# The products of a sample pair with cached values: one key tile for both samples at a time, instead of four key tiles of one sample and then of the other

## The chip, the cores and the metric

The program runs on one core of one Trainium2 chip. The metric is the device time of that core in microseconds (us). The kernel before took 3969.97 us, the median of three runs (3956.18 to 3974.96).

## What is computed

One layer of a hybrid encoder is computed for two groups that share all weights: a prompt of 2048 rows and eight samples of 16 rows each. Each layer projects its input, runs four mixers, adds the result back and ends with a feed-forward block. Three of the four mixers (B, C and D) are attentions. For the samples each has a cache of keys and values from the past, 1024 rows for B and C, 512 for D. Cut to what matters here, for mixer C:

```python
kc = jnp.concatenate([cache['fox_k'], kc], axis=1)      # 1024 cached rows, 16 new ones
vc = jnp.concatenate([cache['fox_v'], vc], axis=1)
...
p = jax.nn.softmax(jnp.where(mask, s, -jnp.inf), axis=-1)
return jnp.einsum('bhqk,bkhd->bqhd', p, v32)
```

The change is in the last product, weights by values, for the samples alone. All numbers are float32.

## The kernel before

The work falls into a dense stream (projections, then the feed-forward block of four parts of the prompt) and a stream of mixers. Both are written as generators. `weave` (line 144) takes a step of the mixers and then dense steps for as long as the mixer's pace says. The result is handed to a scheduler, which fixes the order of each engine's queue before the program runs. An engine then works its own queue strictly from front to back and waits where an operand is missing. All loads and stores stand in one such queue, that of SyncE (SP). In it, too, stand empty instructions that `Order.note` puts there (line 97): each waits for an earlier dense product, and a later dense product waits for it, so a held SP queue can hold TensorE (PE).

The samples' attention runs in three stages, one for each of B, C and D (`attn_samples`, line 1498, called by `mixers`), beside the delta-rule steps of the prompt and the dense stream. `samples_steps` handles the eight samples in four pairs. For a pair, `weights` makes the attention weights, 128 rows: sample `u` of the pair has rows 64u to 64u+63, four heads of 16 queries. Then `values` (line 1602)

- turns the weights into `swT`, one 128x128 tile for each key tile of 128 keys,
- makes the product with the 16 new rows (tile `sxv`) as one full 128-column product, and
- adds the products with the cached values (tile `cv`) in the same PSUM tile, which has the name `ptr`. Each takes 64 columns of `swT` as stationary operand, so sample 0 works in columns 0 to 63 of the array, sample 1 in columns 64 to 127, and both over all 128 rows; 256 value columns stream through.

With `nk` key tiles (8 for B and C, 4 for D) there are 2 x nk products for a pair: 64 in B, 64 in C, 32 in D. They are made in groups of four key tiles:

```python
for s in range(nk // 4):
    for u in range(2):
        v = load(b + u, cv, s, "cv")
        for j in range(4):
            kt = 4 * s + j
            K.pe.matmul(po[64 * u:64 * u + 64, :256], wT[:, kt, 64 * u:64 * u + 64], v[:, j], start=False, stop=(kt == nk - 1))
        yield
```

`load` (line 1549) fetches four key tiles of one sample, 512 KB, from the cache to the tile `cv`, of which there is one buffer, so each load waits for the last product of the group before. The keys have their own tile `ck`, loaded by the same line 1552. `K.pe.matmul` is line 107 in every profile, and `K.pe.transpose` line 110. In the rows below, `d` is the PSUM tile of dense products, and `wu` and `wd` are the weights of the feed-forward block. A float32 product leaves two records on PE, one for each of two passes. A float32r product leaves one.

Elsewhere in the program, `solve` (lines 1319 and 1359) makes four products for the delta rule whose outputs `pw` take turns between the lower and the upper 64 columns (`<-lA,kbv` in the rows); their moving operand has 128 columns.

Of the kernel before, what the change touches and what calls it, by code (L numbers as in the profile page):

```python
# [5 lines left out]
F32 = mybir.dt.float32  # L6
# [3 lines left out]
AF = mybir.ActivationFunctionType  # L10
ALU = mybir.AluOpType
# [4 lines left out]
P = 128  # L16
# [656 lines left out]
def logf_stage(K, part):  # L673

    nc, tc, I, O = K.nc, K.tc, K.I, K.O
    a, b = 4 * part, 4 * part + 4
    with tc.tile_pool(name="lf", bufs=1, side="right", reuse_waits="tile") as sp:
        bf = sp.tile([P, 4], F32, name="bf")
        nc.sync.dma_start(out=bf, in_=I["fox_b_f"].to_broadcast([P, 4]))
        for c, n in [(slice(a, b), 4)] + ([(slice(NP, NT), 1)] if part == 0 else []):  # L680
            x = sp.tile([P, n, 4], F32, name=f"fx{n}")
            nc.vector.tensor_tensor(x, K.fl[:, c], bf.unsqueeze(1).to_broadcast([P, n, 4]), op=ALU.add)
            yield
            sn = sp.tile([P, n, 4], F32, name=f"fsn{n}")
            nc.vector.tensor_scalar(sn, x, 0.0, None, op0=ALU.min)
            l1 = yield from softplus_tail(K, sp, x, [P, n, 4], f"f{n}")
            nc.vector.tensor_tensor(K.logf[:, c], sn, l1, op=ALU.subtract)
        nc.sync.dma_start(out=O["fox_logf_p"].rearrange("(t p) h -> p t h", p=P)[:, a:b], in_=K.logf[:, a:b, :])
        if part == 0:
            nc.sync.dma_start(out=O["fox_logf_s"], in_=K.logf[:, NP, :])  # L690
        yield
        lf = K.logf[:, 0:b, :].rearrange("p t h -> p (t h)")
        n = 4 * b
        pt = K.mps("z")
        K.pe.matmul(pt[:, :n], K.tri, lf, start=True, stop=True)
        po = K.mps("z")
        K.pe.matmul(po[:, :n], K.ones, lf, start=True, stop=True)
        tot = sp.tile([P, b, 4], F32, name="ftot")
        nc.vector.tensor_copy(tot, po[:, :n].rearrange("p (t h) -> p t h", h=4))
        yield  # L700
        inc = sp.tile([P, b, 4], F32, name="finc")
        for h in range(4):
            nc.vector.tensor_tensor_scan(out=inc[:, :, h], data0=tot[:, :, h], data1=K.zeros[:, :b], initial=0.0, op0=ALU.add, op1=ALU.add)
        yield
        nc.vector.tensor_tensor(inc, tot, inc, op=ALU.subtract)
        nf = sp.tile([P, n], F32, name="nf")
        nc.vector.tensor_tensor(nf, inc.rearrange("p t h -> p (t h)"), pt[:, :n], op=ALU.subtract)
        yield
        pf = K.mps("z")
        K.pe.transpose(pf[:n, :P], nf, K.ident)  # L710
        nft = sp.tile([P, P], F32, name="nft")
        nc.vector.tensor_copy(nft[:n], pf[:n, :P])
        nc.sync.dma_start(out=K.nF[4 * a:n], in_=nft[4 * a:n])


def softplus_tail(K, sp, x, shape, tag):

    nc = K.nc
    u = sp.tile(shape, F32, name=tag + "u")
    nc.scalar.activation(u, x, AF.Abs)  # L720
    nc.scalar.activation(u, u, AF.Exp, scale=-1.0)
    yield
    w = sp.tile(shape, F32, name=tag + "w")
    nc.vector.tensor_scalar(w, u, 1.0, None, op0=ALU.add)
    l = sp.tile(shape, F32, name=tag + "l")
    nc.scalar.activation(l, w, AF.Ln)
    yield
    e = sp.tile(shape, F32, name=tag + "e")
    nc.vector.tensor_scalar(e, w, 1.0, None, op0=ALU.subtract)
    nc.vector.tensor_tensor(e, u, e, op=ALU.subtract)  # L730
    nc.vector.reciprocal(w, w)
    nc.vector.tensor_tensor(e, e, w, op=ALU.mult)
    nc.vector.tensor_tensor(l, l, e, op=ALU.add)
    yield
    return l
# [762 lines left out]
def attn_samples(K, g, beside):  # L1498

    A = Ctx()  # L1500
    A.ev, A.wb, A.pb, A.sb = Eng(K.nc, 0.5), 2, 2, 1
    A.psum = lambda: K.mps("ptr")
    A.w = lambda m: A.sp.tile([P, P], F32, name="wn", bufs=1) if m <= P else A.sp.tile([P, 512], F32, name="w", bufs=A.wb)
    with K.tc.tile_pool(name="s" + g, bufs=1, side="right", reuse_waits="tile") as A.sp:
        yield from merge((lab(K.nc, "s" + g, samples_steps(K, A, g)), 1.0), (beside, 1.0))


def samples_steps(K, A, g):
    nc, I, sp, psum = K.nc, K.I, A.sp, A.psum
    gi = "BCD".index(g)  # L1510
    name = {"B": "sb", "C": "fox", "D": "band"}[g]
    ck, cv = I[f"cache_{name}_k"], I[f"cache_{name}_v"]
    nk = 4 if g == "D" else 8
# [3 lines left out]
        segs = segs[::-1]  # L1517
    x0 = []
    for n, src in (("k", K.qs[g]), ("v", K.ks[g])):
        t = sp.tile([P, 4, 256], F32, name="c" + n, bufs=1)[:, 0]  # L1520
        nc.sync.dma_start(out=t, in_=src)
        x0.append(t)
    qn, kn = x0
# [8 lines left out]
    if g == "D":  # L1532
        bias = sp.tile([P, 640], F32, name="sbias", bufs=1)
        for h in range(8):
            r = slice(h * 16, h * 16 + 16)
# [3 lines left out]
    pt = psum()  # L1539
# [3 lines left out]
    for o in range(2):  # L1543
        r = slice(o * 64, o * 64 + 64)
# [1 line left out]
    nc.scalar.copy(kT0.rearrange("p x n -> p (x n)"), pt[:, 256:512])  # L1546
    yield

    def load(b, src, s, tag):

        t = sp.tile([P, 4, 256], F32, name=tag, bufs=1)
        nc.sync.dma_start(out=t, in_=src[0, b, s * 512:(s + 1) * 512].rearrange("(t p) h d -> p t (h d)", p=P))
        return t

    def keys(L, b, s):

        L.kT[s] = []
        for u in range(2):
            k = load(b + u, ck, s, "ck")
            kT = sp.tile([P, 2, 512], F32, name="ckT", bufs=2)  # L1560
            L.kT[s].append(kT)
            for x in range(2):
                pt = psum()
                for j in range(4):
                    K.pe.transpose(pt[:, j * P:(j + 1) * P], k[:, j, x * P:x * P + P], K.ident)
                A.ev.copy(kT[:, x], pt)
                yield

    def weights(L, b):
# [21 lines left out]
        for n, (c0, c1) in enumerate(segs):  # L1591
            if c0 < past and c0 // 512 not in L.kT:
                yield from keys(L, b, c0 // 512)
            if g == "B":
                L.w.segment(c0, c1)
            else:
                L.w.segment(n)
            yield
# [3 lines left out]
    def values(L, b):  # L1602
        w, rl = L.w, None if g == "B" else L.w.rl
        wT = sp.tile([P, nk + 1, P], F32, name="swT", bufs=1)
        for a in range(0, nk + 1, 4):
            e = min(a + 4, nk + 1)
            pt = psum()
            for kt in range(a, e):
                K.pe.transpose(pt[:, (kt - a) * P:(kt - a + 1) * P], w(kt), K.ident)
            A.ev.copy(wT[:, a:e].rearrange("p t n -> p (t n)"), pt[:, :(e - a) * P])  # L1610
            yield
        po = psum()
        K.pe.matmul(po[:, :256], wT[:, nk], vn, start=True, stop=False)
        for s in range(nk // 4):
            for u in range(2):
                v = load(b + u, cv, s, "cv")
                for j in range(4):
                    kt = 4 * s + j
                    K.pe.matmul(po[64 * u:64 * u + 64, :256], wT[:, kt, 64 * u:64 * u + 64], v[:, j], start=False, stop=(kt == nk - 1))
                yield  # L1620
        o4 = sp.tile([P, 4, 64], F32, name="so4", bufs=1)
        nc.vector.tensor_tensor(o4, po[:, :256].rearrange("p (h d) -> p h d", d=64), K.hmask.unsqueeze(2).to_broadcast([P, 4, 64]), op=ALU.mult)
        o = sp.tile([P, 64], F32, name="so", bufs=2)
        nc.vector.tensor_reduce(o, o4.rearrange("p h d -> p d h"), axis=AX.X, op=ALU.add)
        if rl is not None:
            nc.vector.tensor_scalar(o, o, rl, None, op0=ALU.mult)
        sq = sp.tile([P, 64], F32, name="sosq", bufs=1)
        ss = K.small.tile([P, 1], F32, name="soss")
        nc.scalar.activation(sq, o, AF.Square, accum_out=ss)
        r = rsqrt(K, K.small, ss, 1, 1.0 / 64, EPS, "rs1")  # L1630
        yield
        nc.vector.scalar_tensor_tensor(o, o, r, mgr, op0=ALU.mult, op1=ALU.mult)
        for u in range(2):
            dst = K.mixed[SEQ + (b + u) * 16:SEQ + (b + u) * 16 + 16, (1 + gi) * 256:(2 + gi) * 256]
            nc.sync.dma_start(out=dst.rearrange("s (h d) -> h s d", d=64), in_=o[64 * u:64 * u + 64])

    L = Ctx()
    L.kT = {}
    s0 = nk // 4 - 1 if g == "B" else 0
    yield from keys(L, 0, s0)  # L1640
    for b in range(0, NB, 2):
        yield from weights(L, b)
# [391 lines left out]
def gates(K, p):  # L2034

    if p:
        yield from gate_stage(K, 4 * p, 4 * p + 4)
    yield from logf_stage(K, p)
    if p == 2:
        yield from fox_cum_samples(K)  # L2040
# [128 lines left out]
```

## Time and profile before

| | |
|---|---|
| runs | 3974.96, 3956.18, 3969.97 us; median 3969.97 |
| the profiled execution, own time | 3970.47 us |
| its span | 3968.7 us |
| granted TensorE clock, mean over the span | 0.966 |
| PE busy | 3688.0 us (93%) |
| PE weight loads (beside PE) | 3176.5 us (80%) |
| DVE, ACT, POOL busy | 2428.5, 1535.7, 1425.6 us |
| moved by DMA | 830.43 MB, 209 GB/s on average |
| stage B of the samples | about 1180 to 1460 us |
| stage C | about 2030 to 2290 us |
| stage D | about 2925 to 3110 us |

The profiled execution lies 0.5 us from the median, so its span can stand for the runs. A granted clock of 1.0 is 2.4 GHz and one of 0.5 is 1.2 GHz; 0.966 is a mean of stretches at either. The three stages are 725 us of the span; the rest is prompt work and the feed-forward block.

### The profile page before, as it was taken

Reading aid. Unit: us, or ns where it says so; the run is one execution under the profiler, and the core shown is the slowest. Engines: PE = TensorE matmul, PEld = TensorE weight load, DVE = VectorE, ACT = ScalarE, POOL = GpSimd, SP = SyncE. Lnnn points to the kernel's source line nnn. Section 1 sums busy time; section 2 is a strip of 40 time slices with the busy share of each in tenths; the row PEclk is TensorE's granted clock in tenths of the full one; section 3 lists DMA queues with packets and bytes.
Section 4 is the critical chain, followed back from the end, with each engine's and each line's share of the span. In section 5 each row is a group of like instructions: output and inputs, shape, how many; then the busy total and the mean of one; then the engine's idle time right before and its main releaser. Section 6 shows DMA issues by size and latency. Waiting matters only on the chain.

```text
span 3968.7 us, 67360 instructions
## 1 busy us (share of the span) xinstructions
PE 3688.0 (93%) x22763; PEld 3176.5 (80%) x22763; DVE 2428.5 (61%) x5592; ACT 1535.7 (39%) x3351; POOL 1425.6 (36%) x3487
## 2 busy tenths in 40 slices
PE   6988899999988998989889999899899999999999
PEld 4987889989975666767766687788777787899999
DVE  5668655464568756867756568666576644354444
ACT  3455323353355424645533245454343222132221
POOL 4456244362433445742232257411232331121112
PEclk7999999999999999999999999999999999999999
DMA  6887968777786876667656654454655645534442
GB/s 223 290 269 245 305 202 297 272 256 259 235 263 209 286 238 237 204 204 260 210 170 202 210 185 147 152 173 155 214 174 200 207 163 188 205 135 146 146 145 92
DMA packets 528445, 830.43 MB, mean 209 GB/s; under 512 B 112011, under 2 KB 350619, under 8 KB 527836
## 3 DMA queue, kind: packets, MB, share of 16 engines
q1 hardware_dynamic: 526629, 825.16, 62.3%
q8 instruction: 181, 2.97, 0.3%
q0 software_dynamic: 1472, 0.97, 0.1%
q14 instruction: 163, 1.34, 0.1%
HBM read 611.81 MB, written 224.16 MB: 211 GB/s over the span
## 4 chain that ended last, share of the span: by engine, by line
PE 66%; DMA 10%; DVE 8%; POOL 3%; ACT 3%; issue 2%; SPq 1%; DVEq 0%; POOLq 0%; ACTq 0%
PE d L107 47%; PE z L107 6%; PE oT L107 5%; PE ptr L110 4%; PE ptr L107 3%; DVE pr L760 1%; DMA add<-nF 1%; PE d L110 1%; DMA w<-win 1%; DMA raw<-in_w_down_dram 1%; DVE wl L860 1%; DVE gy L1203 1%; PE z L110 1%; DMA wu<-keptw_up 1%; DVE cv L1927 1%
## 5 line engine op out<-in xcount | busy, mean ns | idle before, releaser
L107 PE MATMUL d<-hh,wu 128*128 128x512 f32 (+1 forms) x3520 | 1035.9, 368 | 28.9 <-SPq L97 16.2
L107 PEld LDWEIGHTS d<-hh,wu 128*128 128x128 f32 x3520 | 638.9, 191 | 121.1 <-SPq L97 21.7
L107 PE MATMUL d<-w,hh 128*128 128x256 f32 (+2 forms) x3536 | 683.8, 289 | 28.8 <-DVE w L478 9.9
L107 PE MATMUL d<-hl,wu 128*128 128x512 f32 (+1 forms) x1760 | 650.2, 369 | 25.1 <-SPq L97 23.3
L107 PEld LDWEIGHTS d<-w,hh 128*128 128x128 f32 x3536 | 561.4, 192 | 46.7 <-DVE w L478 12.6
L107 PE MATMUL d<-gh,wd 128*128 128x512 f32 (+1 forms) x1760 | 535.4, 371 | 19.6 <-SPq L97 17.7
L107 PE MATMUL d<-w,hl 128*128 128x256 f32 (+2 forms) x1768 | 504.7, 287 | 0.2 <-DVE hl L427 0.2
L1927 DVE SCALAR_TENSOR_TENSOR cv<-u,fcw,cv 128x512 f32<-128x512 f32 (+1 forms) x440 | 299.2, 703 | 201.4 <-ACT cv L1925 199.1
L1837 DVE SCALAR_TENSOR_TENSOR acc<-d,mod,acc 128x512 f32<-128x512 f32 (+2 forms) x432 | 281.9, 656 | 220.8 <-PE d L107 219.4
L107 PEld LDWEIGHTS d<-hl,wu 128*128 128x128 f32 x1760 | 336.0, 191 | 76.5 <-SPq L97 29.9
L107 PEld LDWEIGHTS d<-gh,wd 128*128 128x128 f32 x1760 | 321.6, 191 | 68.9 <-issue 13.5
L107 PEld LDWEIGHTS d<-w,hl 128*128 128x128 f32 x1768 | 338.6, 192 | 4.8 <-issue 3.3
L107 PE MATMUL d<-gl,wd 128*128 128x512 f32 (+1 forms) x880 | 322.0, 366 | 2.1 <-SPq L97 2.0
L1914 ACT COPY u<-d 128x512 f32<-128x512 f32 (+1 forms) x220 | 110.2, 501 | 486.7 <-PE d L107 478.9
L107 PE MATMUL z<-kT,qT 128*128 128x512 f32 (+3 forms) x864 | 257.4, 382 | 16.0 <-DVE mx L792 10.9
L859 ACT CAST wh<-ptr 128x512 fp32r<-128x512 f32 (+1 forms) x372 | 200.6, 553 | 182.6 <-PE ptr L110 104.9
L860 DVE TENSOR_TENSOR wl<-ptr,wh 128x512 fp32r<-128x512 f32 (+1 forms) x372 | 233.2, 637 | 54.0 <-ACT wh L859 49.5
L1929 POOL COPY hal<-u 128x2 f32<-128x2 f32 x176 | 45.6, 259 | 555.8 <-ACT u L1914 547.6
L110 PE MATMUL ptr<-ident,w 128*128 128x128 f32 x1448 | 230.6, 278 | 14.1 <-POOL pr L755 4.4
L760 DVE TENSOR_TENSOR_SCAN pr<-sn,pr,zeros 128x512 f32<-128x512 f32 (+3 forms) x172 | 220.4, 1287 | 37.2 <-ACT sn L752 31.1
L762 POOL TENSOR_TENSOR w<-w,pr 128x512 f32<-128x512 f32 (+3 forms) x168 | 195.0, 1164 | 87.3 <-DVE pr L760 45.7
L792 DVE CUSTOM_DVE_ANT_0 w<-z,add 128x512 f32<-128x512 f32 (+3 forms) x272 | 147.3, 555 | 110.3 <-PE z L107 54.5
(610 smaller groups left out, 7212.1 us busy)
## 6 DMA issues: line engine op xcount, KB each, us to landing
wu<-keptw_up SPq DMA_DIRECT2D x264, 512.0 KB
w<-win SPq DMA_DIRECT2D x132, 512.0 KB
wd<-keptw_down SPq DMA_DIRECT2D x132, 512.0 KB
keptw_up<-wu SPq DMA_DIRECT2D x88, 512.0 KB
wu<-keptw_o SPq DMA_DIRECT2D x48, 512.0 KB
win<-w SPq DMA_DIRECT2D x44, 512.0 KB
raw<-in_w_up_dram SPq DMA_DIRECT2D x88, 256.0 KB
keptw_down<-wd SPq DMA_DIRECT2D x44, 512.0 KB
```

What stands on the lines that cost most here:

```text
L107: return self.note(self.nc.tensor.matmul(out, lhsT, rhs, **k), n / 2400 * (4 if rhs.dtype == F32 else 1))
L110: return self.note(self.nc.tensor.transpose(*a, **k), 0.107)
L760: nc.vector.tensor_tensor_scan(out=pr[:, 0:m][:, ::-1], data0=sn[:, :m][:, ::-1], data1=K.zeros[:r, :m], initial=carry, op0=ALU.mult, op1= ...
L762: nc.gpsimd.tensor_tensor(w[:, :m], w[:, :m], pr[:, 1:m + 1], op=ALU.mult)
L792: nc.vector.tensor_tensor_reduce(out=w[:, :m], in0=ps[:, :m], in1=self.addend(c0, c1), op0=ALU.add, op1=ALU.max, scale=1.0, scalar=-3.0e38 ...
L859: nc.scalar.copy(wh[:, c0:c1], pt[:, c0:c1])
L860: nc.vector.tensor_tensor(wl[:, c0:c1], pt[:, c0:c1], f(wh[:, c0:c1]), op=ALU.subtract)
L1203: nc.vector.scalar_tensor_tensor(yc, tap(c, i), self.cw[:, c, i:i + 1], yc, op0=ALU.mult, op1=ALU.add)
L1837: nc.vector.scalar_tensor_tensor(acc[k][:, c0:m], ps[:, :m - c0], gate[:, k, 0:1], acc[k][:, c0:m], op0=ALU.mult, op1=ALU.add)
L1914: nc.scalar.copy(u[:, 2 + c0:2 + m], ps[:, :m - c0])
L1927: nc.vector.scalar_tensor_tensor(o, tap(i), cw[:, i:i + 1], o, op0=ALU.mult, op1=ALU.add)
L1929: nc.gpsimd.tensor_copy(K.hal[:, fi], tail)
```

## The change

In `values` the loop goes over key tiles. For each one, both samples' rows are fetched in one load of 256 KB (`load_v`), and the two products follow each other, each on its half of the columns, with its tile position written out. `cv` has two buffers of half the size, together the same 512 KB. The number of products, what they multiply and the bytes loaded stay as they are; there are 80 loads of `cv` instead of 40. A step of the generator now covers two key tiles of both samples instead of four of one, so the number of steps is the same.

Two small tiles go away as well: the sum in `logf_stage` is made in place, and the squares in `values` are written over the first quarter of `so4`, which has been read by then.

```diff
@@ logf_stage
-        nf = sp.tile([P, n], F32, name="nf")
-        nc.vector.tensor_tensor(nf, inc.rearrange("p t h -> p (t h)"), pt[:, :n], op=ALU.subtract)
+        nf = inc.rearrange("p t h -> p (t h)")
+        nc.vector.tensor_tensor(nf, nf, pt[:, :n], op=ALU.subtract)
@@ samples_steps
     for n, src in (("k", K.qs[g]), ("v", K.ks[g])):
-        t = sp.tile([P, 4, 256], F32, name="c" + n, bufs=1)[:, 0]
+        t = sp.tile([P, 4 if n == "k" else 2, 256], F32, name="c" + n, bufs=1 if n == "k" else 2)[:, 0]
...
-    def load(b, src, s, tag):
-
-        t = sp.tile([P, 4, 256], F32, name=tag, bufs=1)
-        nc.sync.dma_start(out=t, in_=src[0, b, s * 512:(s + 1) * 512].rearrange("(t p) h d -> p t (h d)", p=P))
-        return t
+    def load(b, s):
+
+        t = sp.tile([P, 4, 256], F32, name="ck", bufs=1)
+        nc.sync.dma_start(out=t, in_=ck[0, b, s * 512:(s + 1) * 512].rearrange("(t p) h d -> p t (h d)", p=P))
+        return t
+
+    def load_v(b, kt):
+
+        t = sp.tile([P, 2, 256], F32, name="cv", bufs=2)
+        nc.sync.dma_start(out=t, in_=cv[0, b:b + 2, kt * P:(kt + 1) * P].rearrange("u p h d -> p u (h d)"))
+        return t
...
-        for s in range(nk // 4):
+        for kt in range(nk):
+            v = load_v(b, kt)
             for u in range(2):
-                v = load(b + u, cv, s, "cv")
-                for j in range(4):
-                    kt = 4 * s + j
-                    K.pe.matmul(po[64 * u:64 * u + 64, :256], wT[:, kt, 64 * u:64 * u + 64], v[:, j], start=False, stop=(kt == nk - 1))
+                r = 64 * u
+                K.pe.matmul(po[r:r + 64, :256], wT[:, kt, r:r + 64], v[:, u], start=False, stop=(kt == nk - 1), tile_position=(0, r))
+            if kt % 2:
                 yield
...
-        sq = sp.tile([P, 64], F32, name="sosq", bufs=1)
         ss = K.small.tile([P, 1], F32, name="soss")
-        nc.scalar.activation(sq, o, AF.Square, accum_out=ss)
+        nc.scalar.activation(o4[:, 0], o, AF.Square, accum_out=ss)
```

The scheduler makes a new order from this. PE's queue, the first block of products in stage B (`sxv` is the product with the new rows, `ck` are key tiles being transposed). Before:

```order
L107 MATMUL ptr<-sxv,swT 128x256
L107 MATMUL ptr<-cv,swT 64x256 x4
L110 MATMUL ptr<-ident,ck 128x128 x4
L107 MATMUL d<-hl,wu 128x512
L107 MATMUL d<-hh,wu 128x512 x2
L107 MATMUL d<-hl,wu 128x512
L107 MATMUL d<-hh,wu 128x512 x2
L107 MATMUL d<-hl,wu 128x512
L107 MATMUL d<-hh,wu 128x512
L107 MATMUL ptr<-cv,swT 64x256 x4
L107 MATMUL d<-hh,wu 128x512
```

And of the change, with the buffers' numbers:

```order
L107 MATMUL ptr_16679<-sxv_16090,swT_16558 128x256
L107 MATMUL ptr_16679<-cv_16681,swT_16558 64x256 x2
L107 MATMUL ptr_16679<-cv_16685,swT_16558 64x256 x2
L107 MATMUL d_17806<-hh_17733,wu_17794 128x512
L107 MATMUL d_17988<-hh_17733,wu_17976 128x512
L107 MATMUL ptr_16679<-cv_16719,swT_16558 64x256 x2
L110 MATMUL ptr_16700<-ident_123,ck_16697 128x128 x4
L107 MATMUL ptr_16679<-cv_16723,swT_16558 64x256 x2
L107 MATMUL d_17806<-hl_17734,wu_17794 128x512
L107 MATMUL d_17806<-hh_17733,wu_17794 128x512 x2
```

Four products of one sample became two products, one of either sample, from one buffer of `cv`. In all 80 cases the two stand next to each other. There are 66 runs of such products in the new order, 52 of one key tile and 14 of two, with other work of PE between them, where before there were 44 runs.

SP's queue at the same place. Before (`keptw_up` is a store, `raw` a load of the dense stream):

```order
L1552 DMA cv<-in_cache_sb_v_dram 128x4x256
L1813 DMA keptw_up<-wu 128x1024
L1552 DMA cv<-in_cache_sb_v_dram 128x4x256
L1810 DMA raw<-in_w_up_dram 128x4x128
L1552 DMA ck<-in_cache_sb_k_dram 128x4x256
L1237 DMA gK<-kbv 128x768
L1248 DMA gQ<-gqet 128x256
L1552 DMA cv<-in_cache_sb_v_dram 128x4x256
```

And of the change:

```order
L1552 DMA ck<-in_cache_sb_k_dram 128x4x256
L1558 DMA cv<-in_cache_sb_v_dram 128x2x256 x6
L1237 DMA gK<-kbv 128x768
L1552 DMA ck<-in_cache_sb_k_dram 128x4x256
L1558 DMA cv<-in_cache_sb_v_dram 128x2x256
L1248 DMA gQ<-gqet 128x256
L1558 DMA cv<-in_cache_sb_v_dram 128x2x256
```

Six loads of `cv`, each of which waits for an earlier pair of products, now stand in a row, and the store and the load that stood between two of them come after.

## Rows read from the trace of the kernel before

**Rows 1.** The page: the span, busy time by engine, the chain that ended last.
```profile
span 3968.7 us, 67360 instructions
PE 3688.0 (93%) x22763; PEld 3176.5 (80%) x22763; DVE 2428.5 (61%) x5592; ACT 1535.7 (39%) x3351; POOL 1425.6 (36%) x3487
PE 66%; DMA 10%; DVE 8%; POOL 3%; ACT 3%; issue 2%; SPq 1%; DVEq 0%; POOLq 0%; ACTq 0%
```
**Rows 2.** Stretches: us, busy us of each engine (instructions), clock, DMA share, GB/s.
```profile
1180.00:1460.00 280.00, 250.75 (x1239) 177.73 (x1238) 199.88 (x418) 122.77 (x233) 114.30 (x204) 0.95 0.77 253
2030.00:2290.00 260.00, 231.89 (x1211) 165.50 (x1210) 156.82 (x409) 82.49 (x176) 71.63 (x194) 0.95 0.64 202
2925.00:3110.00 185.00, 182.59 (x889) 133.58 (x888) 114.01 (x275) 61.71 (x131) 56.20 (x159) 1.00 0.61 204
3110.00:3968.00 858.00, 837.36 (x5106) 770.15 (x5104) 397.89 (x877) 205.60 (x450) 180.20 (x439) 0.98 0.46 158
```
**Rows 3.** Groups of instructions: busy us, mean ns | idle us before, releaser.
```profile
L107 PE MATMUL ptr<-cv,swT 128*64 128x256 f32 x320 | 79.8, 391 | 6.9 <-DMA cv<-in_cache_fox_v_dram 4.1 <-DMA cv<-in_cache_sb_v_dram 2.8
```
**Rows 4.** PE in order of time, stage B: start, us, tiles, records [idle before].
```profile
1245.29 3.29 PE L107 MATMUL ptr<-cv,swT 128*64 128x256 f32 x8
...
1252.58 1.94 PE L107 MATMUL ptr<-cv,swT 128*64 128x256 f32 x8 [1.58 <-DMA cv<-in_cache_sb_v_dram]
1254.45 0.50 PE L107 MATMUL d<-hh,wu 128*128 128x512 f32 x1
...
1266.40 0.63 PE L107 MATMUL d<-hh,wu 128*128 128x512 f32 x2
1266.87 0.39 PE L107 MATMUL d<-hl,wu 128*128 128x512 f32 x1
1267.19 1.94 PE L107 MATMUL ptr<-cv,swT 128*64 128x256 f32 x8
1269.06 0.66 PE L110 MATMUL ptr<-ident,ck 128*128 128x128 f32 x4
1269.47 0.70 PE L107 MATMUL d<-hh,wu 128*128 128x512 f32 x2
```
**Rows 5.** PE in order of time: 64-column products on alternating halves, and alone.
```profile
493.90 0.43 PE L107 MATMUL ptr<-lA,kbv 128*64 128x128 f32 x2
494.27 0.43 PE L107 MATMUL oT<-kbv,lA 128*128 128x64 f32 x2
...
2259.70 0.66 PE L107 MATMUL oT<-lA,kbv 128*64 128x128 f32 x8
2260.29 0.88 PE L107 MATMUL z<-kbv,lA 128*128 128x64 f32 x6
```
**Rows 6.** The chain of waits: start, us, what; loads of 512 KB to `cv`.
```profile
1248.61 3.93 DMA cv<-in_cache_sb_v_dram
2096.77 3.97 DMA cv<-in_cache_fox_v_dram
2220.13 4.67 DMA cv<-in_cache_fox_v_dram
```
**Rows 7.** The chain of waits: weight loads of 256 KB.
```profile
1177.69 3.49 DMA raw<-in_w_o_dram
1304.06 5.41 DMA raw<-in_w_down_dram
1794.67 6.71 DMA raw<-in_w_down_dram
```
**Rows 8.** Waits in stage B: who waited for what, us in total, times, longest.
```profile
PE d L107 <- SPq L97: 11.5, 4, 7.1
...
SPq L97 <- PE d L107: 71.5, 90, 5.9
SPq L1552 <- PE ptr L107: 19.4, 9, 6.6
```
**Rows 9.** The same in stage C.
```profile
PE d L107 <- SPq L97: 7.7, 4, 4.2
...
SPq L97 <- PE d L107: 92.3, 79, 5.0
```
**Rows 10.** The loads of line 1552: duration on SP in ns, least, median, most.
```profile
L1552 SPq DMA_DIRECT2D cv<-in_cache_sb_v_dram x16: 368/384/1042, 1195.7 to 1450.5; - x16
```

More of the change, by code (lines that the diff above doesn't have):

```diff
@@ L1558, in keys @@
         for u in range(2):
-            k = load(b + u, ck, s, "ck")
+            k = load(b + u, s)
             kT = sp.tile([P, 2, 512], F32, name="ckT", bufs=2)
```

## The prediction

> **What bounds the kernel now.** I read the page first. PE is busy for 3688.0 of 3968.7 us, and the chain that ended last runs through PE for 66% [rows 1]. No other engine passes 61%. The changed products lie in the three stages of the samples' attention, so I read those next, by stretch [rows 2]. PE is busy for 250.75 of 280 us in stage B, 231.89 of 260 in C and 182.59 of 185 in D. After D there are 858 us in which PE works for 837.36, on dense work that stands in its queue. So PE time saved in the stages brings that work forward and is kept to the end, unless something else holds PE in the same stage. D leaves almost no room for that. In B and C PE is idle for a tenth of the time, and there the question is what holds it.
>
> Then the products themselves [rows 3]: 320 records, two for each of 160 products, 79.8 us busy, and 6.9 us of idle time in front of them that a load of `cv` ended. How they follow each other is seen in order of time [rows 4]. A group of four products is eight records; it begins at 1252.58 and the next instruction at 1254.45, so a group holds PE for 1.87 us. All eight records are of one sample and use the same half of the columns, and they stand one behind the other: two products after each other cost twice one.
>
> That two halves need not queue is seen elsewhere in this trace [rows 5]. The delta rule's products have 64 columns over all 128 rows, like ours, stream 128 columns instead of 256, and take turns between the halves. Four of them (eight records) hold PE from 2259.70 to 2260.29, 0.59 us. One alone (two records) holds it from 493.90 to 494.27, 0.37 us. Let a product take p to stream and a run e for changing over. One alone is p + e = 0.37. If the four run two by two, 2p + e = 0.59, so p = 0.22 and e = 0.15; if all four queue, 4p + e = 0.59, so p = 0.07 and e = 0.30. Our own groups, whose products do queue, decide: with twice the columns they should take 4 x 2 x 0.22 + 0.15 = 1.91 us by the first and 4 x 2 x 0.07 + 0.30 = 0.86 by the second, and they take 1.87. So products that take turns between the halves run in twos, and ours stream for (1.87 - 0.15) / 4 = 0.43 us each.
>
> **The products.** Before: 160 x 0.43 + 44 runs x 0.15 = 68.8 + 6.6 = 75.4 us. After: 80 pairs x 0.43 + 66 runs x 0.15 = 34.4 + 9.9 = 44.3 us; the runs are counted in the new order of PE, which keeps every pair together. That is **31.1 us less PE time**, 12.4 each in B and C and 6.2 in D. The first group of stage B takes 3.29 us where others take 1.94 [rows 4], at the lower of the two clocks; with fewer products in it, up to 1.4 us more may go. I leave that to the lower end.
>
> **The waits for `cv`.** Before, the one buffer makes each load wait for the last group. Where it gates PE, 512 KB take 3.9 to 4.7 us [rows 6]; PE's idle time from that is 6.9 us in all [rows 3]. After, the load for key tile k+2 starts when pair k is done, so two loads of 256 KB are under way at a time. I went down the new order's twelve blocks (four in each stage). A pair starts when PE reaches it, or when T + 0.1 us have passed since the pair before the last ended, whichever is later; T is the time from issue to landing. The work between is summed with durations of rows: 0.23 for a dense product, 0.41 for four transposes, from 1269.06 to 1269.47 [rows 4]. The tightest block is the first in B: ahead of its third pair PE has only two dense products, ahead of the fourth four transposes, ahead of the fifth five dense products. Summed over the blocks the waits are 1.7 us at T = 2.0, 10.1 at 3.5, 39 at 5.4 and 68 at 6.7. As a test, the same rule with one buffer and T = 4.0 gives 9.3 us for the kernel before, where the trace has 6.9, so it errs on the high side. T has no row here. The lowest I allow is 2.0, half of what 512 KB take. The highest is a weight load of 256 KB that ran late in stage B, 5.41 us [rows 7]. I take **3.5**, from the 256 KB load at 1177.69 that took 3.49, the nearest in size, time and place. That makes 10.1 - 6.9 = **+3.2 us**, with ends at -5.2 and +32.
>
> The Trainium skill, DMA: Bandwidth & Descriptors, section "Anatomy of one DMA", speaks against halving a load: it gives some 2.0 us for each DMA whatever its size, plus bytes / 436e3 us, a fit for another path of issue. By that formula 512 KB would take 3.2 us, where this trace has 3.9 to 4.7, and 256 KB 2.6; the waits would then be an estimated 3.5 us, and the sum 6.6 us lower than mine. I go by the trace.
>
> **SP.** There are 40 more loads to issue at 0.38 us each [rows 10], 15.4 us in 725 us of stages. SP waits for PE in its empty instructions for 71.5 us in B and 92.3 in C [rows 8, 9], and this covers them. Queued behind a waiting load are other loads, stores and those empty instructions; dense products wait for the latter, now 11.5 us in B and 7.7 in C [rows 8, 9]. SP also waits 19.4 us in B for the one buffer of `cv` or `ck` [rows 8]. With two buffers of `cv` a load comes up earlier, but six now stand in a row in the first block, ahead of a store and a weight load. I take 0; if the cover fails the cost is the 15.4 us of issue, and if half of those 19.2 us of PE's waits go, the gain is some 10 us.
>
> **The rest.** The scheduler also moves other instructions in and between the stages, by places and not in number. I cost this at nothing, and keep for it the same ends as for SP. The sum in place and the squares in `so4` keep their engines and sizes: nothing, since the tiles are free by then.
>
> **The sum.** 3970.0 - 31.1 + 3.2 = 3942.1; I say **3942 us**. The profiled execution's own 3970.5 would give 3942.6.
>
> **The rivals.**
>
> *The loads come late* (0.16). Loads of 256 KB in stage B are seen at 5.41 us [rows 7], and DMA is busy 0.77 there [rows 2]. At T = 5.4 the waits are 39 us, 32 more than now, and the time is 3970 - 31.1 + 32 = 3971: no change. Against it: 512 KB of `cv` themselves take 4 us, and half the bytes to the same tile should not take longer.
>
> *The stages keep half* (0.09). In B and C PE waits on other things a tenth of the time; if half of the 24.8 us saved there turns into longer such waits, the time is 3942 + 12.4 = 3954, no change by the bound below. For it: the empty instructions tie PE to SP. Against it: SP's wait in them is for PE, so a faster PE brings SP forward.
>
> *The halves queue* (0.04). The change then does nothing but cut the runs shorter: 160 x 0.43 + 66 x 0.15 = 78.7 us, 3.3 more than before; with the waits, 3970 + 3.3 + 3.2 = 3977. The Trainium skill, TensorE: Matmul & The Clock Gate, section "Part 3: Packing small matmuls — row/col tiling", says that weight loads overlap running products only where the row groups differ, and here both halves use all rows. By that rule the second product would wait for the first. The products at 2259.70 have the same shape over all rows and took 0.59 us where queuing needs 4 x 0.22 + 0.15 = 1.03 [rows 5], so the trace contradicts it for this case.
>
> *Slower: SP's chain of loads becomes the bound* (0.05). Each load of `cv` stands in SP's queue behind a wait for a pair, and weights stand behind it. If loads take 6.71 us, as one weight load did [rows 7], the waits are 68 us, 61 more than before, and the time is 3970 - 31 + 61 = 4000. It decides from T = 6.3 on, where the waits added pass 31 + 20 us. Against it: no load of `cv` gated PE for more than 4.67 us [rows 6].
>
> **How the numbers follow.** The forecast has 0.66. About 0.5%, 20 us, is what a measurement of this kernel can tell from no change: below 3950 is faster, above 3990 slower. The forecast's bulk is faster; its upper edge, with late loads, half-kept stages and queuing halves, is within the bound: faster 0.67, same 0.28, slower 0.05. The range's lower end is 3970.0 - 31.1 - 5.2 - 10 - 1.4 = 3922. Its upper end takes in the late loads, 3971. Left out are queuing halves, slower, and as much again for orders that fall out badly.
>
> **What would show it.** Right: the `cv` products still have 320 records, but the four records of a lone pair hold PE for about 0.58 us, two starting within 10 ns of each other, and their busy time falls by about 30 us. PE's idle time ended by `cv` loads is 2 to 15 us. PE's busy sum falls to about 3657 us and the stretch after stage D keeps its length. Wrong: a pair holds PE for about 1.0 us (halves queue); idle time ended by `cv` of 30 us and more (late loads); PE's waits for the empty instructions of SP grow beyond 19 us in B and C together while the products shrink as said (the stages keep it).

## The result, and the profile after

The changed kernel takes **3935.54 us**, the median of four runs (3932.53 to 3940.53); the kernel before, run beside it, took 3972.47 (3956.18 to 3975.85). The ratio is 0.9925, with a 95% interval of 0.9905 to 0.9945: faster by 0.75%. Forecast were 3942 us and a gain of 28 us; 37 were gained, and the interval of 22 to 38 us holds both. The products did what was forecast, almost to the letter. PE's idle time did not, and the experiments show that it hangs on the scheduler's order more than on anything that the change set out to do.

The page of the changed kernel: span and busy times.

```profile
span 3930.7 us, 67408 instructions
PE 3664.5 (93%) x22763; PEld 3154.7 (80%) x22763; DVE 2431.6 (62%) x5592; ACT 1537.2 (39%) x3352; POOL 1425.6 (36%) x3487
```

Against [rows 1] the span is 38.0 us shorter and PE is busy 23.5 us less, so 14.5 us went from PE's idle time. The groups of instructions of the changed kernel, the row that answers to [rows 3]:

```profile
L107 PE MATMUL ptr<-cv,swT 128*64 128x256 f32 x320 | 52.0, 419 | 7.8 <-DMA cv<-in_cache_sb_v_dram 7.2 <-DMA cv<-in_cache_fox_v_dram 0.3
```

The same 320 records now cover 52.0 us instead of 79.8; one record is no shorter (419 ns against 391). That is overlap. PE in order of time, the first block of stage B and a run of two key tiles later, against [rows 4]:

```profile
1254.23 0.65 PE L107 MATMUL ptr<-cv,swT 128*64 128x256 f32 x4
1254.81 0.50 PE L107 MATMUL d<-hl,wu 128*128 128x512 f32 x1
...
1300.28 1.08 PE L107 MATMUL ptr<-cv,swT 128*64 128x256 f32 x8
1301.29 0.44 PE L110 MATMUL oT<-ident,gqe 128*128 128x128 f32 x2
```

A lone pair holds PE for 0.58 us (1254.23 to 1254.81) and a run of two pairs for 1.01, which are 0.43 + 0.15 and 2 x 0.43 + 0.15, the two prices of the prediction. The two products of the lone pair start 7 ns apart in the trace.

Who waited, in the changed kernel over the whole span: first PE's waits, then SP's.

```profile
PE d L107 <- SPq L97: 49.7, 30, 11.4
...
PE ptr L107 <- DMA cv<-in_cache_sb_v_dram: 7.2, 3, 5.5
```

```profile
SPq L1558 <- PE ptr L107: 39.1, 43, 2.4
```

And in the kernel before, the same lines:

```profile
PE d L107 <- SPq L97: 61.7, 28, 11.2
```

```profile
SPq L1552 <- PE ptr L107: 60.4, 29, 6.6
```

A load of `cv` or `ck` used to hold SP's queue for up to 6.6 us until the single buffer was free; a load of `cv` now holds it for 2.4 at most, and 39.1 us in all. PE's waits for SP's empty instructions fell by 12.0 us. The one is hardly the cause of the other. In stages B and C, where the loads of `cv` stand, those waits were 11.5 and 7.7 us [rows 8, 9] and are now 13.2 and 4.3. The fall lies between stages B and C, where there are no such loads. There, from 1460 to 2030 us before and from 1460 to 2003 after:

```profile
PE d L107 <- SPq L97: 30.7, 18, 10.6
```

```profile
PE d L107 <- SPq L97: 17.8, 13, 10.0
```

A kernel with one buffer and another order ("before, sample 1 first" below) has 17.2 us between these stages as well.

For the comparisons I cut each profile at the issue of stage B's first load of queries, since nothing ahead of it is changed by the work. The stretch from there to the end, before and after (us, PE busy, then the other engines, clock, DMA share, GB/s):

```profile
1185.40:3968.70 2783.30, 2604.93 (x14517) 2166.82 (x14515) 1699.50 (x3750) 1048.99 (x2262) 899.55 (x2005) 0.97 0.56 188
```

```profile
1182.90:3930.70 2747.80, 2576.81 (x14516) 2137.57 (x14514) 1705.82 (x3750) 1050.60 (x2263) 901.82 (x2005) 0.97 0.58 190
```

It is 35.5 us shorter: 28.1 of PE's busy time, and 178.4 - 171.0 = 7.4 of its idle time. The other 2.5 us lie before stage B, which begins anywhere from 1178.7 to 1186.2 us in the kernels that keep SP's empty instructions.

In stage B itself nothing was gained, as far as the number of records tells. From 1180 to 1460 us PE ran 1238 records where it had run 1239 in [rows 2]; it was busy for 7.6 us less, and so idle for 7.6 us more:

```profile
1180.00:1460.00 280.00, 243.13 (x1238) 166.75 (x1237) 199.28 (x418) 124.72 (x235) 115.26 (x214) 0.93 0.76 246
```

### The profile page after: what moved, and what is told of

It is laid out like the page before. It is cut to its first block, busy times and chain, and to the rows that moved or that the text cites. A ratio compares the mean times of both kernels' runs of the same rounds, so it can differ in the third digit from the quotient of the medians.

```text
span 3930.7 us, 67408 instructions
## 1 busy us (share of the span) xinstructions
PE 3664.5 (93%) x22763; PEld 3154.7 (80%) x22763; DVE 2431.6 (62%) x5592; ACT 1537.2 (39%) x3352; POOL 1425.6 (36%) x3487
## 4 chain that ended last, share of the span: by engine, by line
PE 62%; DMA 10%; DVE 10%; POOL 4%; ACT 3%; issue 3%; SPq 1%; DVEq 0%; POOLq 0%; ACTq 0%
PE d L107 45%; PE z L107 5%; PE oT L107 5%; PE ptr L110 4%; PE ptr L107 2%; PE d L110 1%; DVE pr L760 1%; DMA w<-win 1%; DMA add<-nF 1%; DVE acc L1842 1%; DVE gy L1203 1%; DVE wl L860 1%; PE z L110 1%; DMA raw<-in_w_up_dram 1%; DVE cv L1932 1%
## 5 line engine op out<-in xcount | busy, mean ns | idle before, releaser
L107 PE MATMUL d<-w,hh 128*128 128x256 f32 (+2 forms) x3536 | 684.7, 289 | 28.1 <-DVE w L478 9.5
L107 PEld LDWEIGHTS d<-hl,wu 128*128 128x128 f32 x1760 | 334.8, 190 | 66.0 <-SPq L97 17.2
L110 PE MATMUL ptr<-ident,w 128*128 128x128 f32 x1448 | 227.7, 276 | 15.3 <-POOL w L762 3.9
L809 ACT ACTIVATE w<-w,nm 128x512 f32<-128x512 f32 (+3 forms) x284 | 174.1, 616 | 105.6 <-DVE nm L802 82.6
```

The source lines that it names most:

```text
L107: return self.note(self.nc.tensor.matmul(out, lhsT, rhs, **k), n / 2400 * (4 if rhs.dtype == F32 else 1))
L110: return self.note(self.nc.tensor.transpose(*a, **k), 0.107)
L809: self.K.nc.scalar.activation(w, w, AF.Exp, bias=self.nm, accum_out=self.l[:, s:s + 1])
```

## The experiments

Three theories stood at the start. A: the halves run beside each other, and that is the gain. B: the gain lies in the half-sized loads with two buffers. C: the scheduler's new order is lucky. Each profile is split as above; all the numbers stand in one table behind the experiments.

**Both samples on the same half.** The changed kernel, with its loads and buffers, but

```diff
-                r = 64 * u
-                K.pe.matmul(po[r:r + 64, :256], wT[:, kt, r:r + 64], v[:, u], ..., tile_position=(0, r))
+                r = 64 * u if kt == nk - 1 else 0
+                K.pe.matmul(po[r:r + 64, :256], wT[:, kt, 64 * u:64 * u + 64], v[:, u], ..., tile_position=(0, r))
```

> The changed kernel with the products of both samples put on the lower half of the columns, except those of the last key tile; loads, buffers and the number of products stay. (Sample 1's sums land in sample 0's rows, so the samples' attention outputs are not the reference's.) Theory A, the halves run beside each other and that is the gain: 68 of 80 pairs now queue, each holds PE 0.43 us longer, 29 us in all, so about 3965 us, and a lone pair holds PE for 1.0 us instead of 0.58. Theory B, the gain is in the half-sized loads with two buffers: about 3936 us, as the changed kernel. Theory C, the gain is the luck of a new order: anywhere between the two, with product records as in A.

Measured: 3945.56 us against 3965.83, ratio 0.9939 (0.9925 to 0.9953). The products queue as theory A says, in the groups of instructions and in PE's order of time:

```profile
L107 PE MATMUL ptr<-cv,swT 128*64 128x256 f32 x320 | 79.0, 395 | 2.8 <-DMA cv<-in_cache_sb_v_dram 1.7 <-DMA cv<-in_cache_fox_v_dram 1.1
```

```profile
1312.21 1.08 PE L107 MATMUL ptr<-cv,swT 128*64 128x256 f32 x4
```

Four records cover 1.08 us instead of 0.65. But the time is 20 us under the kernel before, where theory A wanted no gain and theory B all of it. From stage B on:

```profile
1186.20:3945.80 2759.60, 2603.88 (x14517) 2161.42 (x14515) 1702.57 (x3750) 1050.37 (x2263) 889.63 (x2005) 0.97 0.59 190
```

PE's busy time is that of the kernel before, within 1.1 us; its idle time is 155.7 us instead of 178.4. So there are two accounts. The halves settle the busy one. Something else moves the idle one. Against the changed kernel PE is busy for 27.1 us more and idle for 15.3 us less, and the intervals of the two ratios overlap, so this pair alone does not show what the halves are worth in time.

**Small loads, no turns.** The kernel before, with 256 KB loads in two buffers:

```diff
-                v = load(b + u, cv, s, "cv")
-                for j in range(4):
-                    kt = 4 * s + j
-                    K.pe.matmul(...)
+                for j in range(0, 4, 2):
+                    v = load_v(b + u, 4 * s + j)
+                    for kt in (4 * s + j, 4 * s + j + 1):
+                        K.pe.matmul(...)
```

> The kernel before with loads of 256 KB and two buffers of cv, but each load of two key tiles of one sample, and the products one sample after the other as before; no turns. Theory A: 160 x 0.43 + 66 x 0.15 = 78.7 us of products, 3.3 more than before, waits for cv about as in the changed kernel (7.8 against 6.9): about 3974 us, no gain. Theory B: about 3936 us. Theory C: a gain or a loss of some 10 us without a cause in the products.

Measured: 3956.54 us, ratio 0.9974 (0.9962 to 0.9986). PE's busy time is 2605.34 us, as before; idle 162.7. Neither A nor B: a quarter of a per cent, all of it idle time. It is what C allows, and what a smaller effect of the buffers would do.

**One buffer, with turns.** This is the kernel before, without the two small edits. Four products of two key tiles take turns, and the one buffer holds both tiles of both samples. Against the changed kernel, the tile and its loads (cut):

```diff
-        t = sp.tile([P, 2, 256], F32, name="cv", bufs=2)
+        t = sp.tile([P, 4, 256], F32, name="cv", bufs=1)
+        for u in range(2):
+            nc.sync.dma_start(out=t[:, 2 * u:2 * u + 2], ...)
```

> The products take turns between the samples as in the change, but one buffer of cv holds two key tiles of both samples (512 KB, fetched in two loads), so no load runs ahead. The order breaks one turn in nineteen of the forty groups (one product, other work, then three). Theory A: 20 x 1.01 + 20 x (0.58 + 1.01) = 52 us of products against 75.4 before, so 23 us less, and waits for cv of 7 to 15 us as before or a little more: 3945 to 3955 us. Theory B: no gain, about 3970 us, with the waits of the kernel before. Theory C: no statement.

Measured: 3945.73 us, ratio 0.9941 (0.9926 to 0.9956), as theory A has it. Busy 2579.96 us, 25 less than before; idle 179.0, as before. Together with the two above this looked like two clean effects, halves for busy time and two buffers for idle time.

**The two small edits alone** (the sum in place, the squares over `so4`, in the kernel before):

> The kernel before with the two small edits alone: the sum of logf_stage in place and the squares written over so4; the scheduler makes a new order of it. Theories A and B: about 3970 us, within 5 us of the kernel before. Theory C, a new order by itself moves the time: 10 us or more away from the kernel before, either way.

Measured: 3967.69 us, ratio 0.9999 (0.9987 to 1.0012). They do nothing, and idle time is 178.8. That says little on theory C: in the traces, PE's records of this kernel follow each other as in the kernel before in all but 4 of 22763 places, by the names of the tiles.

**The other sample first.** The changed kernel with one edit that only makes the scheduler order things anew:

```diff
-            for u in range(2):
+            for u in (1, 0):
```

> The changed kernel with sample 1's product ahead of sample 0's in each pair; the scheduler makes a new order of it, nothing else changes. Theory A (halves side by side) and the finding that two half-sized buffers save PE idle time both say: as the changed kernel, 3930 to 3942 us, with PE's idle time from stage B on at 150 to 170 us. Theory C (order luck): 10 us or more off the changed kernel's 3935.5.

Measured: **3959.10 us**, ratio 0.9975 (0.9963 to 0.9988); 24 us slower than the changed kernel by the medians, 20 by the ratios, with the same work. From stage B on, and two rows of its waits:

```profile
1182.90:3956.90 2774.00, 2576.52 (x14516) 2142.27 (x14514) 1700.05 (x3750) 1047.64 (x2263) 883.82 (x2005) 0.97 0.58 189
```

```profile
PE ptr L107 <- DMA cv<-in_cache_sb_v_dram: 11.1, 6, 4.9
...
PE ptr L110 <- DMA ck<-in_cache_band_k_dram: 8.4, 2, 4.4
```

Busy time is that of the changed kernel within 0.3 us, and idle time 197.5 us instead of 171.0. So C has a share after all: an order can take back most of the gain. Waits for `cv` grow by 4.9 us over the changed kernel's row above (7.8 in all there, 12.7 here), and keys come late.

**Without SP's empty instructions.** They are left out in the kernel before, in the small-loads kernel and in the changed one:

```diff
-            if self.dense and "proj3" in self.K.done and "mix3" not in self.K.done:
+            if False and self.dense and "proj3" in self.K.done and "mix3" not in self.K.done:
```

> The kernel before without the empty SP instructions of Order.note and the waits that hang on them (they set the pace of loads and carry no data). No theory sets its time, it is the base for the next two; PE's waits for SP at line 97 must be gone, which were 61.7 us over the span and some 19 in stages B and C.

Measured: 3951.93 us, ratio 0.9956 (0.9942 to 0.9969). The waits at line 97 are gone.

> The small-loads kernel (256 KB, two buffers, one sample after the other) without the empty SP instructions. Theory D, two buffers help because a load of cv holds SP's queue for less time and PE waits less at SP's empty instructions: no gain is left here, within 5 us of the kernel before without them. Theory E, two buffers help because cv, keys and weights themselves arrive earlier: still some 10 us faster than that kernel, PE idle from stage B on some 15 us lower.

Measured: 3962.04 us, ratio 0.9983 (0.9971 to 0.9996): 10 us slower than the same without small loads, which speaks against theory E, under which the data itself arrives earlier. Theory D wanted them within 5 us, so it isn't confirmed either. Nor is a difference of 10 us beyond what an order alone can do, as the changed kernel with sample 1 first showed.

> The changed kernel without the empty SP instructions. Theory D: faster than the kernel before without them by the products alone, 20 to 27 us. Theory E: faster than it by 30 to 37 us, as with them.

Measured: **3927.43 us**, ratio 0.9898 (0.9879 to 0.9918), 24.5 us faster than the kernel before without them, inside theory D's 20 to 27. Busy time is 27.0 us less (2580.55 to 2553.55). Idle time from stage B on is 176.5 us in the kernel before, 182.2 with small loads and 181.0 in the changed kernel, so here two buffers save none. It is the fastest of all; its interval and the changed kernel's overlap. Why the kernel before gains 15 us without those instructions wasn't followed up.

**Four more orders.** To see whether idle time follows the buffers (F) or the order alone (L), four kernels were given a new order by an edit that changes no work. The small-loads kernel with its samples in the other sequence:

> The small-loads kernel with the two samples' halves of each step in the other sequence; a new order, the same work. All theories: PE's work without idle time as in the small-loads kernel, some 5 us over the kernel before. Theory F, two half-sized buffers save 10 to 20 us of PE idle time: 3950 to 3960 us, idle from stage B on at 150 to 165 us. Theory L, the idle time is luck of each order: idle anywhere from 150 to 195 us, time from 3950 to 3990.

The changed kernel with its step ended after even key tiles (`if kt % 2 == 0: yield`):

> The changed kernel with the step of the generator ended after even key tiles instead of odd ones; a new order, the same work. All theories: PE's work some 25 us under the kernel before. Theory F: 3930 to 3945 us, idle from stage B on at 150 to 170 us. Theory L: idle anywhere from 150 to 195 us, time from 3925 to 3965.

The kernel before with sample 1 first:

> The kernel before with sample 1's group of four products ahead of sample 0's; a new order, the same work, one buffer. All theories: PE's work as in the kernel before. Theory F: 3962 to 3975 us, idle from stage B on at 170 to 178 us, like the three other kernels with one buffer. Theory L: idle anywhere from 150 to 195 us, time from 3945 to 3990.

And the kernel with both samples on one half, with that same step:

> The kernel with both samples on the lower half (the last key tile excepted; the samples' attention outputs are again not the reference's), with the step ended after even key tiles; beside the other run of this call that ends the step there, the halves are the difference. All theories: PE's work some 25 us over that run's. Theory F: also 20 to 28 us slower than that run. Theory L: slower by 25 us, give or take 20.

Measured, in that sequence: 3955.90 us (ratio 0.9971, 0.9960 to 0.9982), 3933.28 (0.9917, 0.9904 to 0.9931), 3960.51 (0.9984, 0.9974 to 0.9995), 3948.26 (0.9951, 0.9938 to 0.9963). All from stage B on; idle is the length of the stretch less PE's busy time:

| kernel | buffers of cv | products | PE busy, us | PE idle, us | ratio |
|---|---|---|---|---|---|
| before | 1 | queue | 2604.9 | 178.4 | 1 |
| small edits alone | 1 | queue | 2603.8 | 178.8 | 0.9999 |
| before, sample 1 first | 1 | queue | 2598.2 | 171.3 | 0.9984 |
| small loads | 2 | queue | 2605.3 | 162.7 | 0.9974 |
| small loads, sample 1 first | 2 | queue | 2600.8 | 170.8 | 0.9971 |
| same half | 2 | queue | 2603.9 | 155.7 | 0.9939 |
| same half, other step | 2 | queue | 2595.6 | 160.4 | 0.9951 |
| one buffer with turns | 1 | in twos | 2580.0 | 179.0 | 0.9941 |
| **changed** | 2 | in twos | 2576.8 | 171.0 | 0.9925 |
| changed, other step | 2 | in twos | 2572.9 | 171.8 | 0.9917 |
| changed, sample 1 first | 2 | in twos | 2576.5 | 197.5 | 0.9975 |

Each row is one profiled execution, and executions of one kernel differ: the kernel before took from 3954.88 to 3975.61 us in 17 runs, and the one profiled of "before, sample 1 first" (3950.28 us) was the fastest of 11. Idle times less than some 10 us apart are therefore not told apart. The ratios rest on several runs each.

The busy column falls into two groups that don't touch: 2595.6 to 2605.3 where the products queue, 2572.9 to 2580.0 where they run in twos. The means are 2601.8 and 2576.5, 25 us apart, in whatever order. That is theory A's term, shown.

The idle column doesn't. With products that queue, two buffers have 155.7 to 170.8 us against 171.3 to 178.8 with one: 0.5 to 23 us, always the same way. With products in twos the sign is open: 171.0, 171.8 and 197.5 with two buffers, 179.0 with one. Sample 1 first moved it by 7 us in the kernel before, by 8 in the small-loads kernel and by 26.5 in the changed one; by the ratios the time moved by 6, 1 and 20 us. So F holds at most as a tendency where the products queue (ratios of 0.9939 to 0.9974 with two buffers, 0.9984 to 1 with one), and L in size: an order moved the time by 1 to 6 us, and once by 20.

The two kernels with the other step were timed side by side. There the turns gain 3948.26 - 3933.28 = 15.0 us (13.5 by the ratios, give or take 7): 22.7 us less busy time, and 11.4 us more idle time. (The profiles begin stage B 3.7 us apart, which makes up the difference.) PE's waits for the loads of `cv` in stage B are 9.0 us with turns and 1.8 on the same half, those for SP at line 97 50.4 and 38.9; others offset a part of that. The first two kernels of the kind, changed and same half, show the same: 27.1 us less busy time and 15.3 us more idle time. So about half of the saved busy time came back as idle time in both. That shorter products leave less PE work to cover the loads is a likely reason, but not a shown one, since the order differs within both pairs too: some 3000 of PE's 22763 records stand elsewhere.

## Why the prediction was right, and where it wasn't

- *PE time saved is kept to the end.* Right in direction: PE's busy time from stage B on fell by 28.1 us and the stretch by 35.5. It isn't kept in full by itself: with the halves as the only difference in the work, about half came back as idle time, twice; with one buffer all of the 25 us were kept, and without the empty instructions 24.5 of 27.0. The work after stage D kept its length in one sense: PE's last 5110 records take 855.7 us, where its last 5106 took 858.0 [rows 2]. But the last product of `cv` moved from 3102.6 to 3027.0 us, twice as far as the end of the program, so dense work that had stood ahead of it now follows.
- *Products: 31.1 us less.* Right, a little high: 28.1 us between the two profiles, 25 between the groups of the table. The price of a pair, 0.58 us, is exact; it came from the delta rule's products of the same shape in the profile before [rows 5]. The busy span of the group fell by 27.8. PE's busy sum became 3664.5 us and not 3657, as 4.6 us of busy time more stand ahead of stage B.
- *Waits for cv: +3.2 us at T = 3.5.* 6.9 became 7.8, 0.9 more [rows 3]. Two other orders of the changed kernel had 9.6 and 12.7, and one buffer with turns 6.8, so the range given was fair, and its middle a matter of order. But the rule behind it is not what happened. One wait makes up 5.5 of the 7.8 us, here in PE's order of time and then in the chain of waits:

```profile
1423.19 1.97 PE L107 MATMUL ptr<-cv,swT 128*64 128x256 f32 x8 [5.48 <-DMA cv<-in_cache_sb_v_dram]
```

```profile
1417.86 5.29 DMA cv<-in_cache_sb_v_dram
```

The pairs before it had ended at 1415.15 us, and by the rule the load starts then and takes 3.5 us. It started 2.7 us later, behind two stores and a weight load in SP's queue, and took 5.29.
- *SP: 0.* About right for what it was meant for, the stages: PE's waits at line 97 in B and C were 19.2 us and are 17.5, and the sign of being wrong, more than 19, was not seen. The 12.0 us less over the span lie between the stages, where the new order is at work and no load of `cv` is. What SP's queue did cost is in the late load above.
- *The rest, the new order: 0.* This is the term that was missing: PE's idle time fell by 7.4 us, and nothing in the products, the loads or the buffers is shown to have done it. As the middle of a wide spread 0 may stand; its ends of some 10 and 15 us were too narrow, with 26.5 us of idle time and 20 us of time seen between two orders of the same work.
- *The Trainium skill, DMA: Bandwidth & Descriptors, section "Anatomy of one DMA"*, by whose formula the waits would have been an estimated 3.5 us: the changed kernel's 7.8 lies nearer to the 10.1 that came from this trace's rows. The three loads of stage B that ended a wait of PE took 2.73, 4.34 and 5.29 us in the chain of waits, all above the 2.6 of the formula for 256 KB.
- *The rivals.* That the halves queue is refuted by the pair's 0.58 us against 1.01 on one half. That loads come late needed 39 us of waits for `cv`; 7.8 were seen. That SP's chain of loads becomes the bound would have needed 58 or more; SP's hold by such a load shrank instead. That the stages keep half, with a chance of 0.09, came close to true: 15.3 of 27.1 and 11.4 of 22.7 us in the two pairs that differ in the halves, and stage B of the changed kernel shows no gain at all. In the total this was covered by idle time saved elsewhere.

So the forecast of 28 us stood for 31.1 kept and 3.2 lost, and the 38 us between the two profiles are some 28 of products, 7 of idle time and 2.5 ahead of stage B. The saving of the products is shown. That the total came out near the forecast is in part luck, since the stages did not keep that saving as forecast and the order made up for it. The changed kernel with sample 1 first, with the same idea in it, was only 0.25% faster than the kernel before, some 8 to 10 us.

## What to carry to other kernels

Float32 products with 64-column stationary operands should take turns between the halves of the array: a pair then costs little more than one, and the price can be read from any alternating pair that the trace already has. Split each comparison into the busy engine's work and its idle time before believing a gain of half a per cent: the work is stable, while a scheduler's new order alone moved idle time here by 7 to 26 us between single profiles, and the time by 1 to 20 us. Try a few orders that change no work, both to judge an idea and to pick the best one.

## What the runs showed of the hardware that was not expected

The two halves give exactly 0.43 us a pair beside a 0.15 us changeover, in each of the blocks shown, at a granted clock of 1.0 (at 0.5 a lone pair took 1.05 us, from 1249.69 to 1250.74), at no cost in the length of a record (391 and 419 ns on average, the latter with the first, longer records of more runs). No contention between the two streams of 128 rows was seen. The Trainium skill, TensorE: Matmul & The Clock Gate, section "Part 3: Packing small matmuls — row/col tiling", lets weight loads overlap running products only where the row groups differ. This case does not bear that out. Here are the weight loads (PEld) of a pair, in the changed kernel and then with both samples on one half:

```profile
1254.23 0.20 PEld L107 LDWEIGHTS ptr<-cv,swT 128*64 128x64 f32 x4 [0.36 <-issue]
```

```profile
1312.20 0.62 PEld L107 LDWEIGHTS ptr<-cv,swT 128*64 128x64 f32 x4 [0.24 <-issue]
```

All of them use all rows, and in both kernels they lie beside the products shown above for 1254.23 and 1312.21 us. So weight loads overlap products on two halves and on one; what the halves decide is whether the products themselves overlap, 0.58 us against 1.01. The prediction inferred from that sentence that the second product would have to wait. But the sentence is on weight loads, and the section's table of measured speed-ups has column tiles in it too.
